# In-projection of a hybrid DeltaNet / neighbourhood-attention layer: values stored four tiles at a time, window copies, a norm's bank, query squares and a triangle mask moved

## The chip, the cores and the metric

The kernel runs on one core of one Trainium2 chip. The metric is the time of one execution in microseconds (us), measured on the device. Times without the profiler are the median of three runs. One more execution was recorded by the hardware profiler, and every view quoted here comes from it.

The core has a matrix engine (TensorE, in the profile PE, its weight loads PEld), a vector engine (DVE), a scalar engine (ACT), a general engine (POOL), and SP, which here only issues DMA transfers. Each engine runs its own list of instructions in order. They wait for each other through semaphores. PE writes its results into banks of an accumulator memory, and the other engines have to copy them out (evacuate them) before a bank is used again.

## The reference

One layer over 1024 latent tokens and 256 context tokens of width 1024. The part that matters here is the input projection, whose columns feed two groups:

```python
px = modulate(rms_norm(x, norm1_w[i]), sh1, sc1) @ w_in[i]
pc = modulate(rms_norm(ctx, norm1_w[i]), csh1, csc1) @ w_in[i]
...
# group A, gated DeltaNet: q, k, v through a short convolution and SiLU
q = l2_normalize(q) * DN_HEAD_DIM ** -0.5
k = l2_normalize(k)
...
m = jnp.where(strict, jnp.einsum("bhncd,bhnmd->bhncm", kb, k) * decay, 0.0)
a_mat = jnp.eye(CHUNK, dtype=f32) + m
u = lax.linalg.triangular_solve(a_mat, v * beta[..., None], left_side=True, lower=True, unit_diagonal=True)
...
# group B, neighbourhood attention
q = rms_norm(q, q_norm_w) * NA_HEAD_DIM ** -0.5
k = rms_norm(k, k_norm_w)
```

Then follow the scans over chunks (group A), the attention over windows of 8 rows (group B), the output projection and a SwiGLU feed-forward network.

## The kernel before

The projection is a list of jobs, worked off in the loop near the end of the printed code. A Block job computes 128 columns of w_in for all tokens; its matmuls are those of L390. The operands are split in two parts each (hh and hl for the tokens, whi and wlo for the weights), and three products are added, so a Block has for each of eight k-steps three products in three pieces of 256, 512 and 512 columns, 72 matmuls (48 in q and nq, which have two pieces). The kinds are k, q, v of group A and nk, nq of group B. A Wide job computes 264 or 256 columns with the tokens as the other operand, ten tiles of 128 tokens each, 24 matmuls L581 per tile: the values of group B (nv, in two halves) and the gate z. The order of jobs is k0 to k3, the values' half 1, nk0 to nk2, the values' half 0, nk3, nq0 to nq2, q0 to q3, then z and v blocks and nq3.

While a job's matmuls run, pieces of other work are put between them, one per step, as Python generators: the convolution's taps of the job before (`taps`, DVE), the finishing of a job (`finish`, transposes and products of keys, L520 and L542), and two backgrounds. `bg2` holds `modulation`, which multiplies the later modulation weights (tile wad, loaded by L213, added up on DVE by L234, summed by PE at L219). `bg` holds `block_inverses` and then `preps`. `block_inverses` builds decay tables (rc on POOL L796, PE L809), transposes them (L828, evacuated by ACT L830), inverts all 32 x 32 diagonal blocks in 30 pairs of steps on DVE (L838, L840), transposes back (PE L850) and stores x_d (L860, L863). `preps` prepares the scan's chunks: it loads e, kk and xc (L890 to L892), masks e to a triangle on POOL (L902), takes its exponential on ACT (L911), and multiplies on PE into bank pr (L920 and L929; L922 evacuates L920's result). A `yield` ends a piece.

What comes out is the order of the instructions on each engine. Banks: blk has four, m and pr two each. The norm of a nk block (L485) squares, sums with a constant matrix and takes logarithm and exponential on ACT; its three pieces all use m.

Small tiles share buffers by tag. Tag kx has three buffers of 640 KB each, for vt, kk, kd (of a k block's finish), kTh, the norm's hl16, and z4. The tag zt has two buffers of one tile of values (128 x 264): ACT copies a tile into it (L592) and SP stores it to nv_d (L595). After the values' half 0, sixteen copies from nv_d to vw_d (L1037) arrange the windows for the attention. All of SP's transfers are issued in one order.

## Time and profile before

| | |
|---|---|
| median of 3 runs | 1564.35 us (1562.84 to 1565.23) |
| profiled execution | 1570.02 us |
| its span (first to last instruction) | 1568.2 us |
| mean granted clock of PE | 0.979 |
| PE busy in the span | 1473.0 us (94%) |
| in-projection | about 37 to 560 us of the span |

The profile lists engines' busy time, their waits (who ended the idle time before an instruction), and the granted clock of PE, in shares of full speed. A timeline row gives the start, the time that a run of like instructions takes, the engine, line, operation, output and input, and in brackets the idle time before it and what ended it. "SPq" rows are transfers issued by SP. L followed by a number is the line of the kernel before; the changed kernel's lines are given where they are used.

### The profile page before, as it was taken

How to read it: one execution, taken by the hardware profiler on the slowest of the kernel's cores; microseconds unless marked ns; L12 is line 12 of the kernel's file. 1: busy time of each engine (PE TensorE's matmuls, PEld its weight loads, DVE VectorE, ACT ScalarE, POOL GpSimd, SP SyncE). 2: the span in 40 equal slices, each digit the busy share in tenths (PEclk: the TensorE clock that was granted, in tenths of full speed). 3: DMA queues.
4: the chain of work that ended last, by engine and by line, in shares of the span. 5: the costliest groups of instructions: out<-in, count | busy, mean ns of one | idle time of the engine just before them, and what ended most of it. 6: DMA issues, size and time to landing. Idle time of an engine off the chain costs nothing.

```text
span 1568.2 us, 23886 instructions
## 1 busy us (share of the span) xinstructions
PE 1473.0 (94%) x8535; PEld 1228.2 (78%) x8535; DVE 1000.3 (64%) x1877; ACT 721.1 (46%) x1406; POOL 185.6 (12%) x253
## 2 busy tenths in 40 slices
PE   3999998999999989899979989999999999999999
PEld 1789777777988868787867878888888888888887
DVE  4866479345264665678986469855555556689642
ACT  5443262684356345566753265333333334445441
POOL 1043710342043300000000000000000000000000
PEclk9999899999999999999998999999999999999999
DMA  9457133654468489899639402533323224698742
GB/s 368 132 191 229 46 85 114 218 166 144 155 217 248 154 226 307 262 287 280 199 97 303 177 29 78 194 108 116 101 101 101 101 101 146 222 369 308 236 153 82
DMA packets 214503, 280.50 MB, mean 179 GB/s; under 512 B 16288, under 2 KB 120304, under 8 KB 213360
## 3 DMA queue, kind: packets, MB, share of 16 engines
q1 hardware_dynamic: 213520, 278.34, 54.4%
q8 instruction: 67, 1.10, 0.3%
q10 hardware_dynamic: 864, 0.63, 0.1%
q14 instruction: 52, 0.43, 0.1%
HBM read 212.02 MB, written 71.08 MB: 181 GB/s over the span
## 4 chain that ended last, share of the span: by engine, by line
PE 67%; ACT 4%; DMA 4%; DVE 3%; issue 2%; POOL 1%; SPq 1%; DVEq 0%; POOLq 0%; ACTq 0%
PE ps L1232 27%; PE ps L1579 13%; PE blk L390 6%; PE ps L1363 4%; PE blk L581 3%; PE sc L318 2%; PE sc L308 2%; PE sc L296 2%; PE pr L929 2%; PE ps L1125 1%; PE ps L1385 1%; PE pr L920 1%; PE ps L1137 1%; PE ps L1142 1%; PE ps L1106 1%
## 5 line engine op out<-in xcount | busy, mean ns | idle before, releaser
L390 PE MATMUL blk<-hh,whi 128*128 128x512 f32 (+1 forms) x416 | 125.5, 396 | 9.9 <-ACT zt L592 5.7
L1293 ACT CAST uhi<-ws 128x512 fp32r<-128x512 f32 x91 | 54.8, 624 | 150.0 <-PE ps L1232 71.3
L1293 ACT CAST uhi<-wq 128x512 fp32r<-128x512 f32 x101 | 60.7, 622 | 135.6 <-issue 61.3
L390 PE MATMUL blk<-hh,wlo 128*128 128x512 f32 (+1 forms) x416 | 117.7, 379 | 2.3 <-POOL wlo L200 2.3
L390 PE MATMUL blk<-hl,whi 128*128 128x512 f32 (+1 forms) x416 | 116.4, 378 | 0.0
L1294 DVE TENSOR_TENSOR ulo<-wq,uhi 128x512 fp32r<-128x512 f32 x101 | 67.4, 688 | 66.1 <-ACT uhi L1293 36.0
L1232 PE MATMUL ps<-hT,uhi 128*128 128x512 f32 x336 | 104.6, 392 | 3.2 <-ACT hT L1411 3.1
L1232 PE MATMUL ps<-lT,uhi 128*128 128x512 f32 x336 | 103.8, 390 | 0.0
L1232 PE MATMUL ps<-hT,ulo 128*128 128x512 f32 x336 | 103.4, 389 | 0.0
L390 PEld LDWEIGHTS blk<-hh,whi 128*128 128x128 f32 x416 | 70.4, 195 | 25.6 <-ACT zt L592 6.0
L1232 PE MATMUL ps<-hB,uhi 128*128 128x512 f32 x288 | 89.7, 392 | 0.0
L390 PEld LDWEIGHTS blk<-hh,wlo 128*128 128x128 f32 x416 | 74.4, 195 | 19.3 <-POOL wlo L200 2.8
L1232 PE MATMUL ps<-lB,uhi 128*128 128x512 f32 x288 | 89.3, 391 | 0.0
L1232 PE MATMUL ps<-hB,ulo 128*128 128x512 f32 x288 | 88.8, 389 | 0.0
L581 PE MATMUL blk<-zhi,hh 128*128 128x264 f32 (+1 forms) x288 | 85.3, 296 | 0.0
L390 PEld LDWEIGHTS blk<-hl,whi 128*128 128x128 f32 x416 | 74.2, 194 | 14.1
L1294 DVE TENSOR_TENSOR ulo<-ws,uhi 128x512 fp32r<-128x512 f32 x91 | 60.8, 687 | 36.1 <-ACT uhi L1293 27.8
L581 PE MATMUL blk<-zhi,hl 128*128 128x264 f32 (+1 forms) x288 | 82.8, 287 | 0.0
L581 PE MATMUL blk<-zlo,hh 128*128 128x264 f32 (+1 forms) x288 | 82.4, 286 | 0.0
L1232 PEld LDWEIGHTS ps<-hT,uhi 128*128 128x128 f32 x336 | 63.1, 189 | 16.9 <-ACT hT L1411 3.5
L1232 PEld LDWEIGHTS ps<-lT,uhi 128*128 128x128 f32 x336 | 63.4, 189 | 13.3
L1232 PEld LDWEIGHTS ps<-hT,ulo 128*128 128x128 f32 x336 | 63.2, 188 | 13.2
(331 smaller groups left out, 3555.0 us busy)
## 6 DMA issues: line engine op xcount, KB each, us to landing
wq<-w_fo SPq DMA_DIRECT2D x99, 256.0 KB
wq<-w_gu SPq DMA_DIRECT2D x88, 256.0 KB
wad<-wa SPq DMA_DIRECT2D x64, 256.0 KB
bt<-rpb SPq DMA_DIRECT2D x64, 192.0 KB
t_d<-g SPq DMA_DIRECT2D x22, 512.0 KB
fr<-t_d SPq DMA_DIRECT2D x44, 256.0 KB
f_d<-g SPq DMA_DIRECT2D x33, 256.0 KB
fr<-f_d SPq DMA_DIRECT2D x33, 256.0 KB
```

Of the source, the lines that this page charges most:

```text
L296: pe.matmul(sc[:, u * 640 + n0:u * 640 + n1], q, ks[i], start=i == 0, stop=i == 1)
L308: pe.transpose(sc[:, u * 640 + j * 128:u * 640 + (j + 1) * 128], bt[:, j * 128:(j + 1) * 128], ident)
L318: pe.matmul(sc[u * ND:u * ND + ND, 1280:1408], vv, pt[:, j * 128:(j + 1) * 128], start=j == 0, stop=j == 4)
L390: pe.matmul(o, ww[:, k], xx[k][:, s], start=k == 0 and j == 0, stop=k == KT - 1 and j == end)
L581: pe.matmul(p[:, :c1 - c0], x[k][:, s], ww[:, k, c0:c1], start=k == 0 and j == 0, stop=k == KT - 1 and j == 2)
L920: pe.matmul(p[:, h * 128:h * 128 + 96], kk[:, h], fx[:, h, s], start=True, stop=True)
L929: pe.matmul(p[q, h * 128:h * 128 + 32 * r], f[:, h, q], y[:, h, s], start=True, stop=True)
L1232: pe.matmul(o, w[wi][:, k], x[xi][:, k], start=first and k == 0 and j == 0, stop=k == n - 1 and j == 2, skip_group_check=True)
L1293: act.copy(hi, self.raw[key])
L1294: dve.tensor_tensor(lo, self.raw[key], hi.bitcast(F32), OP.subtract)
L1363: pe.matmul(o, w[wi][:, k], parts[xi][k][:, s], start=k == 0 and j == 0, stop=k == KT - 1 and j == 2)
L1579: pe.matmul(o[b], w[wi][:, b], F[xn, p][xi], start=n in (0, 1, 5) and p == 0 and j == 0, stop=p == NFB // 2 - 1 and j == 2, skip_group_che ...
```

## The change

1. The values' tiles go into one tile nv4 of four tiles (128 x 4 x 264) of tag kx, stored when four are full (and after the last two): three stores per half instead of ten. The tag zt is gone.
2. The sixteen copies of vw_d become a generator `windows`, stepped twice per k-step in the blocks after the values' half 0.
3. The third piece of a nk norm takes its bank from pr instead of m.
4. The query squares' sum (eight matmuls and a copy, L479 and L481) moves from `norm` to `finish`, behind the load of kTh, with a yield of its own.
5. The triangle mask (L902) moves out of `prep` and is issued one item ahead.
6. Two more yields stand ahead of the loop over `cuts` in `block_inverses`.
7. In the loop of a Wide job `bg2` makes three steps instead of two.

```diff
@@ -474,14 +474,9 @@
                 r = self.r
                 if kind == "q":
                     sp.dma_start(qT_d[:, i], acc[:, t0:])
-                    p = bank()
-                    for c in range(8):
-                        pe.matmul(p[:, c:c + 1], r[:, t0 + c * 128:t0 + (c + 1) * 128], M[C_ONE][:, 0:1],
-                                  start=True, stop=True)
-                    dve.tensor_copy(SQ[:, :, i], p[:, 0:8])
                     return
                 for s0, n in self.segs:
-                    p = bank()
+                    p = bank("pr" if kind == "nk" and s0 >= 768 else "m")
                     pe.matmul(p[:, :n], M[C_BD2], r[:, s0:s0 + n], start=True, stop=True)
                     act.activation(r[:, s0:s0 + n], p[:, :n], AF.Ln, bias=b_eps, scale=1.0 / ND)
                 if kind == "nq":
@@ -529,6 +524,12 @@
                 if kind == "q":
                     kT = cp.tile([128, T], F32, name="kTh", tag="kx", bufs=3)
                     sp.dma_start(kT, kT_d[:, i])
+                    p, r, t0 = bank(), self.r, self.t0
+                    for c in range(8):
+                        pe.matmul(p[:, c:c + 1], r[:, t0 + c * 128:t0 + (c + 1) * 128], M[C_ONE][:, 0:1],
+                                  start=True, stop=True)
+                    dve.tensor_copy(SQ[:, :, i], p[:, 0:8])
+                    yield
                 else:
                     kT = acc
                 if kind in "kq":
@@ -588,11 +589,15 @@
                     nv = 248 if half else 264
                     for t in range(NCH):
                         p = self.wide(t, 0, 264)
-                        vt = cp.tile([128, 264], F32, name="zt", tag="zt", bufs=2)
-                        act.copy(vt[:, :nv], p[:, :nv])
+                        if t % 4 == 0:
+                            vt = cp.tile([128, 4, 264], F32, name="nv4", tag="kx", bufs=3)
+                        act.copy(vt[:, t % 4, :nv], p[:, :nv])
                         if half:
                             act.copy(ab[:, t], p[:, 248:264])
-                        sp.dma_start(nv_d[t * 128:(t + 1) * 128, half * 264:half * 264 + nv], vt[:, :nv])
+                        if t % 4 == 3 or t == NCH - 1:
+                            t0 = t // 4 * 4
+                            sp.dma_start(nv_d[t0 * 128:(t + 1) * 128, half * 264:half * 264 + nv]
+                                         .rearrange("(c p) d -> p c d", p=128), vt[:, :t + 1 - t0, :nv])
                         yield
                     return
                 for t in range(2, NCH):
@@ -801,6 +806,8 @@
                         return out
 
                     nxt = rhs(*cuts[0])
+                    yield
+                    yield
                     yield
                     for i, (d, u0, n) in enumerate(cuts):
                         rcs, nxt = nxt, rhs(*cuts[i + 1]) if i + 1 < len(cuts) else None
@@ -898,9 +905,6 @@
 
                 def prep(n, d, c, kk, xc, e, at):
                     lat = c >= 2
-
-                    pool.affine_select(e, e, pattern=[[0, 4], [1 - 2 * d, 128]], compare_op=OP.is_ge, fill=-1.0e30,
-                                       base=0, channel_multiplier=2 * d - 1)
                     y, fx = ys[n % 4], fxs[n % 2]
                     for b in range(4):
                         q = slice(b * 32, b * 32 + 32)
@@ -931,6 +935,14 @@
                         yield 1
                     stores.append((y_d[d, c], y, tick[0] + 2))
 
+                def triangle(item):
+
+                    (d, _, _, _, e, _), made = item
+                    if not made:
+                        pool.affine_select(e, e, pattern=[[0, 4], [1 - 2 * d, 128]], compare_op=OP.is_ge, fill=-1.0e30,
+                                           base=0, channel_multiplier=2 * d - 1)
+                        item[1] = True
+
                 stores, tick = [], [0]
 
                 def flush(n):
@@ -942,10 +954,13 @@
                 n = 0
                 while live or todo or landing:
                     while len(landing) < 2 and todo and (todo[0][1] < 2 or all(x in done for x in queries)):
-                        landing.append(fetch(*todo.pop(0)))
+                        landing.append([fetch(*todo.pop(0)), False])
                     if landing and len(live) < 3:
-                        live.append(prep(n, *landing.pop(0)))
+                        triangle(landing[0])
+                        live.append(prep(n, *landing.pop(0)[0]))
                         n += 1
+                        if landing:
+                            triangle(landing[0])
                     if not live:
                         yield
                     nxt = []
@@ -968,6 +983,15 @@
         values = inv + 3
         queries = range(turn - 1, later)
         jobs += [Wide("z", 0, zp), Block("v", 0), Wide("z", 1, zp), Block("v", 1), Block("v", 2), Block("v", 3), Block("nq", 3)]
+
+        def windows():
+            vlat = nv_d[CT:].rearrange("(r c) d -> r c d", c=64)
+            for cb in range(4):
+                for ch in range(4):
+                    sp.dma_start(vw_d[:, cb, ch], vlat[4 * ch:4 * ch + 4, BLKS[cb]:BLKS[cb] + 32])
+                    yield
+
+        copies = Background()
 
         def blk(n):
             return jobs[n] if 0 <= n < len(jobs) and isinstance(jobs[n], Block) else None
@@ -1012,7 +1036,7 @@
                         fin = nrm.finish()
                         done.add(n - 1)
                         nrm = None
-                    bg2.step(2)
+                    bg2.step(3)
                     if n < turn:
                         bg.step(2)
                     if n >= turn:
@@ -1026,15 +1050,13 @@
                         next(fin, 0)
                     bg.step(1 if n < turn else 3)
                     bg2.step(1)
+                    copies.step(2)
                 j.evac()
             for _ in fin:
                 pass
             done.add(n - 2)
             if isinstance(j, Wide) and n == values:
-                vlat = nv_d[CT:].rearrange("(r c) d -> r c d", c=64)
-                for cb in range(4):
-                    for ch in range(4):
-                        sp.dma_start(vw_d[:, cb, ch], vlat[4 * ch:4 * ch + 4, BLKS[cb]:BLKS[cb] + 32])
+                copies.add(windows())
             if nrm:
                 nrm.norm()
             if isinstance(j, Block) and j.later is None:
```

Since the order on each engine is a result of all of this, these rows show what stands in it now, at three places. In the rows, a name with a number is one tile of that name, and x4 means four times in a row.

First, SP's list in the values' half 1 (before; wad are the modulation's weights, nv_d the values, kk_d and k_d the keys' products and transposes):

```order
L213 DMA wad<-wa 128x512 x2
L595 DMA nv_d<-zt 128x248
L472 DMA kT_d<-cacc 128x1280
L213 DMA wad<-wa 128x512 x2
L555 DMA kk_d<-kk 1280x1x128
L595 DMA nv_d<-zt 128x248
L213 DMA wad<-wa 128x512 x2
L595 DMA nv_d<-zt 128x248
L213 DMA wad<-wa 128x512 x2
L595 DMA nv_d<-zt 128x248
L528 DMA k_d<-vt 128x10x128
```

and SP's list there in the changed kernel:

```order
L599 DMA nv_d<-nv_957 128x4x248
L213 DMA wad<-wa 128x512 x3
L523 DMA k_d<-vt 128x10x128
L213 DMA wad<-wa 128x512 x3
L472 DMA kT_d<-cacc 128x1280
L556 DMA kk_d<-kk 1280x1x128
L213 DMA wad<-wa 128x512 x2
L599 DMA nv_d<-nv_1142 128x4x248
L523 DMA k_d<-vt 128x10x128
L599 DMA nv_d<-nv_1313 128x2x248
```

The last loads of wad now stand directly behind the store of kk_d, and they are the last two, where four were behind it before; the stores of values are fewer. PE's list at the end of that job, before (L219 sums a modulation product, L542 multiplies keys, L390 begins nk0):

```order
L581 MATMUL blk<-zlo,hh_418 128x264
L542 MATMUL m<-cacc 128x128 x6
L219 MATMUL m<-ones,acc_1165 128x1 x4
L390 MATMUL blk<-hh_134,whi 128x256
L390 MATMUL blk<-hh_134,whi 128x512 x2
```

and the same sum, the last of the modulation, in the changed kernel (L515 is L520 of before):

```order
L582 MATMUL blk<-zlo,hh_418 128x264
L515 MATMUL m<-cst,cacc 128x128 x2
L219 MATMUL m<-ones,acc_1071 128x1 x4
L582 MATMUL blk<-zhi,hh_134 128x264
L582 MATMUL blk<-zhi,hl_135 128x264
```

It moved from the job's end to the end of its eighth tile, ahead of two more tiles.

Second, PE's list in the last k-steps of block nk2, before (L828 is the last of four groups of transposes that feed the block inverses):

```order
L390 MATMUL blk<-hl_415,whi 128x256
L390 MATMUL blk<-hl_415,whi 128x512 x2
L390 MATMUL blk<-hh_414,wlo 128x256
L390 MATMUL blk<-hh_414,wlo 128x512 x2
L828 MATMUL m<-cst,WK 80x128 x8
L390 MATMUL blk<-hh_416,whi 128x256
L390 MATMUL blk<-hh_416,whi 128x512 x2
```

and in the changed kernel, where L835 is L828 of before and L480 is L485:

```order
L390 MATMUL blk<-hh_418,wlo 128x256
L390 MATMUL blk<-hh_418,wlo 128x512 x2
L835 MATMUL m<-cst,WK 80x128 x8
L480 MATMUL pr<-cr,cst 128x512
L480 MATMUL m<-cr,cst 128x256
L480 MATMUL m<-cr,cst 128x512
L582 MATMUL blk<-zhi,hh_134 128x264
```

The feeding transposes moved back by two k-steps (18 matmuls L390), the last of them to the block's end; the norm's one piece has a bank pr.

Third, PE's list in block q2, before (the query squares of q0):

```order
L390 MATMUL blk<-hh_418,wlo 128x512 x2
L390 MATMUL blk<-hh_134,whi 128x512 x2
L390 MATMUL blk<-hl_135,whi 128x512
L479 MATMUL m<-ones,cr 128x1 x8
L390 MATMUL blk<-hl_135,whi 128x512
L390 MATMUL blk<-hh_134,wlo 128x512 x2
```

and in the changed kernel (L529 is L479 of before, L543 is L542):

```order
L390 MATMUL blk<-hl_141,whi 128x512 x2
L390 MATMUL blk<-hh_140,wlo 128x512 x2
L529 MATMUL m<-ones,cr 128x1 x8
L390 MATMUL blk<-hh_412,whi 128x512 x2
L390 MATMUL blk<-hl_413,whi 128x512 x2
L390 MATMUL blk<-hh_412,wlo 128x512 x2
L543 MATMUL m<-cacc,kTh 128x128 x4
```

They moved from the third matmul of the block to behind its fourth k-step.

## The prediction

> **What bounds the kernel now.** I read the engines' totals first, then what TensorE (PE) waited for in the in-projection, then the clock by stretches of 40 us there.
>
> ```profile
> PE 1473.0 (94%) x8535; PEld 1228.2 (78%) x8535; DVE 1000.3 (64%) x1877; ACT 721.1 (46%) x1406; POOL 185.6 (12%) x253
> ```
>
> PE is busy for 94% of the span, so only its own idle time and a lowered clock can be won without removing matmuls, and the change removes none. Everything it moves runs between 113 and 560 us. PE's waits from 37 to 560 us (released by; total, times, longest):
>
> ```profile
> PE blk L390 <- ACT zt L592: 5.7, 1, 5.7
> PE m L485 <- ACT cr L486: 5.2, 4, 1.5
> PE pr L929 <- ACT kk L922: 3.5, 2, 3.0
> PE m L479 <- ACT cr L464: 3.4, 1, 3.4
> PE m L219 <- DVE modp L221: 2.1, 1, 2.1
> PE m L809 <- POOL rc L796: 2.0, 1, 2.0
> ```
>
> These six make 21.9 us, and each belongs to one edit. A wait also costs what comes after it. Two groups of the same one-column matmuls in PE's timeline, sixteen records each (start, busy, what, idle before), and two rows of the block matmuls:
>
> ```profile
> 360.66 3.57 PE L479 MATMUL m<-ones,cr 128*128 128x1 f32 x16 [3.36 <-ACT cr L464]
> ...
> 376.38 0.62 PE L390 MATMUL blk<-hh,whi 128*128 128x512 f32 x2
> 376.83 0.62 PE L390 MATMUL blk<-hl,whi 128*128 128x512 f32 x2
> ...
> 377.74 1.84 PE L479 MATMUL m<-ones,cr 128*128 128x1 f32 x16
> ```
>
> After a gap of 3.36 us they took 3.57 us, without a gap 1.84: half speed. The stretches of 40 us show how much (the number behind the engines is the granted clock, PEclk):
>
> ```profile
> 120.00:160.00 40.00, 36.79 (x291) 36.06 (x290) 26.79 (x39) 12.20 (x37) 15.79 (x20) 0.95 0.67 207
> 160.00:200.00 40.00, 36.65 (x172) 29.42 (x172) 20.20 (x44) 14.15 (x26) 24.44 (x23) 0.93 0.18 59
> 240.00:280.00 40.00, 34.35 (x203) 30.45 (x203) 33.76 (x38) 9.09 (x13) 2.41 (x1) 0.91 0.33 117
> 360.00:400.00 40.00, 39.34 (x223) 35.11 (x224) 20.27 (x18) 14.03 (x20) 9.53 (x4) 0.91 0.45 151
> 440.00:480.00 40.00, 36.97 (x313) 34.00 (x313) 24.20 (x35) 25.53 (x60) 19.65 (x31) 0.91 0.70 220
> ```
>
> 40 us times the missing clock is 2.0, 2.8, 3.6, 3.6 and 3.6 us, and each of these stretches holds one of the long waits. So a long wait costs itself and 2 to 3.6 us of half speed.
>
> **The change part by part**, in the times of the profiled execution (1570.02 us; span 1568.2), which is 5.67 us above the unprofiled median of 1564.35.
>
> *First values block (half 1, 113 to 157 us).* The new tiles nv4 take buffers of tag kx, which has three, shared with vt, kk and kd. SP, ACT, POOL, DVE and PE rows of before:
>
> ```profile
> 126.33 0.57 SPq L555 DMA_DIRECT2D kk_d<-kk  x1
> 132.59 0.43 SPq L528 DMA_DIRECT2D k_d<-vt  x1
> 142.68 0.56 SPq L555 DMA_DIRECT2D kk_d<-kk  x1
> 144.15 1.87 SPq L213 DMA_DIRECT2D wad<-wa  x2
> 137.64 0.59 ACT L522 COPY vt<-m 128x512 f32<-128x512 f32 x1 [0.50 <-DMA k_d<-vt]
> 135.62 2.93 POOL L547 TENSOR_TENSOR kd<-kk,cst 128x1280 f32<-128x1280 f32 x1 [9.32 <-ACT kk L543]
> 151.36 3.11 DVE L234 SCALAR_TENSOR_TENSOR acc<-wad,sc,acc 128x512 f32<-128x512 f32 x4 [7.62 <-DMA wad<-wa]
> 127.48 1.05 PE L542 MATMUL m<-cacc 128*128 128x128 f32 x8
> ...
> 143.17 0.38 PE L520 MATMUL m<-cst,cacc 128*128 128x128 f32 x2
> 154.62 1.02 PE L219 MATMUL m<-ones,acc 128*128 128x1 f32 x8 [2.12 <-DVE modp L221]
> 156.73 1.44 PE L390 MATMUL blk<-hh,whi 128*128 128x256 f32 x3 [1.09 <-ACT kk L543]
> ```
>
> A 640 KB store freed its buffer 137.64 − 132.59 = 5.0 us after its issue. Now job k2's vt lies where k1's kk was, so its copies wait for the store issued at 126.33: about 131, and PE's L542 of 127.48 comes about 3.4 us later. k2's kd then waits for k2's k_d store (from the same 5.0 us, an estimate: until 141.5), and takes 2.9 us; the zeroing behind it ends near 146, and the kk_d store is issued then instead of at 142.68. The last two wad loads stand behind it on SP. Before, such loads were used 151.36 − 144.15 = 7.2 us after issue; now that is about 153 to 154. bg2.step(3) moves the last L219 on PE from the block's end to the place of the L520 that ran at 143.17, so PE arrives there near 146 and waits until about 154. Behind L219 are still 48 matmuls L581 and the transposes, 7.4 us. Job nk0 starts near 161.5 instead of 156.73: **+4.8**, with half speed behind the wait as before. Ends: −4.1 if the buffers come free in time (2.1 and the 2.0 of clock), +9.8 if the loads also wait out one more store (5.0).
>
> *Two more yields, first consequence.* POOL's pieces for L809 were late because of a cast of the values weights:
>
> ```profile
> 185.44 3.69 POOL L574 TENSOR_TENSOR zlo<-wraw,zhi 128x1056 fp32r<-128x1056 f32 x1
> ```
>
> The last L809 now stands 18 L390 later on PE (about 4 us, as two L390 start every 0.45 us), which covers the 2.0. With the 2.8 of clock that is up to −4.8; some of the lost clock may stem from nk0's start: **−3.0** (−4.8 to 0).
>
> *Norm piece in bank pr.* The first three blocks' third piece no longer waits for a bank m: −1.4 for the first; the next two are in the following sum.
>
> *Values four at a time, and the block inverses.* ACT's wait for nv_d stores and with it PE's 5.7 goes. But the inverse's chain on DVE is next (30 pairs, then the row where PE picks up its result):
>
> ```profile
> L838 DVE TENSOR_TENSOR tt<-N 80x120 f32<-80x120 f32 (+14 forms) x30 | 27.5, 915 | 7.1 <-ACT N L830 6.1
> L840 DVE TENSOR_TENSOR N<-N,tt 80x120 f32<-80x120 f32 (+14 forms) x30 | 25.4, 847 | 0.9
> 213.50 1.07 ACT L830 COPY N<-m 80x512 f32<-80x512 f32 x2 [1.56 <-PE m L828]
> 274.99 0.28 DVE L840 TENSOR_TENSOR N<-N,tt 80x120 f32<-80x120 f32 x1
> 281.84 0.34 PE L850 MATMUL m<-cst,N 80*128 80x80 f32 x2
> ```
>
> From the last L830 (214.57) to the chain's end (275.27) it is 60.7 us, and PE came 6.6 us after that. Now the feeding matmuls L828 stand 18 L390 later (4.2 us): end 279.5. PE reaches L850, itself moved 16 L390 (3.6 us) back, at 281.84 + 3.6 − 5.7 − 3.6 (clock) − 1.5 − 1.0 (the two norms) = 273.6, so it **waits about 6 us for DVE**, and restarts at half speed (2.5). Against 285.4 before: 279.8 + 2.5, **−3.1**. Ends: −11.8 without the new wait, 0 if ACT brings the result later still.
>
> The sixteen copies to vw_d aren't spread by SP's order: four, three and nine stand behind the three stores. They waited before too, beside PE's work, and their cover is the whole stretch to the next weights:
>
> ```profile
> 264.48 13.23 SPq L1037 DMA_DIRECT2D vw_d<-nv_d  x6
> ```
>
> *nk3's third piece.* The fourth wait (1.3) goes, but with the scan's products taking pr first, the piece is 86 L390 later on PE. ACT's and DVE's steps on it release the buffer cacc, and nq1's evacuation L423 needs that buffer and must be done before q0's first L390:
>
> ```profile
> 294.56 1.12 PE L485 MATMUL m<-cr,cst 128*128 128x512 f32 x2 [1.27 <-ACT cr L486]
> ...
> 300.82 1.26 ACT L498 CAST hl<-cacc 128x1280 f16<-128x1280 f32 x1 [1.62 <-DVE cacc L493]
> ...
> 316.25 1.09 ACT L423 ACTIVATE cacc<-blk 128x512 f32<-128x512 f32 x2
> ...
> 332.48 1.03 PE L390 MATMUL blk<-hh,whi 128*128 128x512 f32 x2
> ```
>
> Before, the evacuation was done 332.48 − 317.3 = 15.1 us ahead. Now the piece stands only 6 L390 and some small products (estimate 3.6 us) ahead of q0. From the piece to the cast's end took 302.1 − 294.6 = 7.5 us, and DVE's subtraction and half the evacuation add some 1.9: 9.4 us. So PE **waits about 5.8 us** there, and a little at a lower clock: 6.5 (0 to 10), **+5.2** net (−1.3 to +8.7).
>
> *Query squares.* Eight matmuls and one DVE copy go from norm to finish, behind the kTh load; no DMA moves with them. In PE's row they now come 21 L390 later (4.8 us), longer than the wait of 3.36: 3.4 and 3.6 of clock go, and I keep 1 for the first: **−6.0** (−7.0 to −3.4).
>
> The Trainium skill ("TensorE: Matmul & The Clock Gate", section "HAM oscillation — how this bites in real kernels") says that PE must have no idle gap over about 3.4 us. By it only the 5.7 us wait would lower the clock, and the 3.6 would not be there to win; this trace disagrees, with half speed right behind 3.36 us and a clock of 0.93 around a wait of 2.0. The sum goes by the rows.
>
> *Triangle.* The mask L902 stood behind a weight cast on POOL, the exponential behind the mask on ACT, and the copy that PE waited for behind that:
>
> ```profile
> 448.13 3.33 POOL L200 TENSOR_TENSOR wlo<-wraw,whi 128x1024 fp32r<-128x1024 f32 x1 [2.03 <-ACT whi L199]
> 452.26 0.40 ACT L911 ACTIVATE e<-e,GN 128x128 f32<-128x128 f32 x1 [3.40 <-POOL e L902]
> ```
>
> Now the mask is ahead of that cast and L922 no longer behind a waiting L911: 3.0 and 3.6 of clock, **−6.6** (to 0 if POOL's copies ahead of it wait for a store).
>
> Sum: 4.8 − 3.0 − 1.4 − 3.1 + 5.2 − 6.0 − 6.6 = −10.1. Profiled 1559.9, unprofiled **1554.2 us**, 0.6% less.
>
> **Rivals.**
> - *The kx buffers come free in time and nq1's evacuation isn't late.* First block −4.1, L809 −4.8, nk3 −1.3, squares −7.0, the rest as above: −28.3, 1536.0 us. For it: the DMA engines were only 0.67 busy there (the figure behind PEclk), so stores might land sooner. Against: the 5.0 us row. Without DVE's bound too it would be 1527.
> - *New waits for old, nothing won.* The mask still waits (0 instead of −6.6) and the squares' clock isn't regained (−3.4 instead of −6.0): −0.9, 1563.5 us. For it: vw_d is still bunched, and DVE's chain shows how near the next wait lies.
> - *Slower: stores in the first values block.* If in the three-buffer ring vt, nv4 and kd each wait out a store one after another, at 5.0 us each with PE idle, four of them make 20 us. The gain without that block is 14.9; above a loss of 18.0 there the change is over 0.2% slower, and with 20 it is at 1569.5. Against it: ten tiles give PE 30 us of work beside them.
> - *The clock drops only past 3.4 us:* L809, squares and triangle then give their waits alone, −1.2, −2.4 and −3.0 instead of −3.0, −6.0 and −6.6, in sum −1.1: 1563.3 us. The half speed of L479 behind 3.36 us speaks against it. It is the Trainium skill's rule named above.
>
> **How the numbers follow.** Forecast 0.58 (its own range 1547 to 1561), first rival 0.16, no gain 0.13, slower 0.11, clock 0.02. Faster by over 0.2% (3.1 us, about what a measurement of this kernel can tell from no change) 0.74, within 0.15, slower 0.11. The range 1537 to 1565 takes in the forecast, the cases without gain and the nearer part of the first rival; it leaves out the slower one and half the first.
>
> **What would show it.** Right: PE's list has no zt, no L485 and no 3.4 us row for the squares; it has a wait of 4 to 8 us on DVE at the moved L219 and one of 3 to 6 us at L850's new line, one of 4 to 8 us in front of q0, and clocks near 1.00 around 360 and 450 us. Wrong: L219 without a wait (first rival), a wait over 10 us at the first block (slower), or nq1's evacuation done before PE reaches q0.

## The result, and the profile after

The changed kernel takes 1569.78 us (median of 15 runs, 1564.43 to 1575.60) against 1565.23 (1558.24 to 1568.27) for the kernel before: ratio 1.0037, 95% interval 1.0026 to 1.0048. It is slower by 0.37%, about 5.8 us by the ratio (the two medians differ by 4.6). The prediction said 0.6% faster and is wrong in sign, and the median lies above its range.

The waits that the change aimed at are gone. PE's waits of the changed kernel from 37 to 560 us (waiting, released by; total, times, longest):

```profile
PE m L219 <- DVE acc L234: 7.4, 1, 7.4
PE m L857 <- DVE N L851: 5.7, 1, 5.7
PE m L857 <- ACT WK L859: 3.5, 1, 3.5
PE pr L933 <- DVE y L934: 2.8, 4, 1.2
...
PE pr L924 <- DVE y L934: 2.2, 1, 2.2
PE pr L924 <- DVE kk L916: 2.0, 1, 2.0
...
PE m L543 <- ACT vt L517: 1.6, 1, 1.6
PE m L816 <- POOL rc L801: 1.0, 1, 1.0
...
PE blk L390 <- ACT cacc L423: 0.8, 1, 0.8
```

No row is left for the values' copies, the key norms or the query squares, and the longest wait for the copy kk of L926 (L922 before) is 1.0 us instead of 3.0. But L219 waits 7.4 us where it waited 2.1, and the pickup of the inverse (L857, formerly L850) waits 5.7 and 3.5 us where it waited not at all. The same stretches of 40 us as in the prediction, and the one between 280 and 320 us (PEclk is the third figure from the end):

```profile
120.00:160.00 40.00, 31.07 (x241) 30.65 (x241) 22.60 (x33) 9.69 (x28) 12.96 (x19) 0.91 0.67 208
160.00:200.00 40.00, 38.33 (x214) 32.82 (x212) 20.13 (x47) 10.75 (x25) 22.52 (x21) 0.96 0.16 51
...
280.00:320.00 40.00, 29.01 (x128) 22.63 (x129) 14.38 (x20) 17.34 (x34) 11.55 (x18) 0.87 0.54 181
320.00:360.00 40.00, 37.46 (x208) 27.10 (x207) 17.39 (x27) 35.72 (x74) 19.07 (x33) 0.87 0.62 177
360.00:400.00 40.00, 40.00 (x212) 34.26 (x211) 22.86 (x20) 20.91 (x28) 8.98 (x5) 1.00 0.49 157
...
440.00:480.00 40.00, 36.78 (x338) 32.70 (x338) 25.08 (x39) 25.46 (x56) 20.79 (x32) 1.00 0.75 243
```

The clock that was low around 260, 360 and 450 us is now low in two stretches from 280 to 360 us: 40 us times 0.13, twice, is 10.4 us, where the kernel before had lost nothing. In steps of 10 us this is not one long stretch but three places:

```profile
280.00:290.00 10.00, 4.56 (x24) 3.91 (x24) 5.83 (x13) 1.63 (x4) 0.00 (x0) 0.66 0.39 141
290.00:300.00 10.00, 6.49 (x28) 4.72 (x27) 2.74 (x2) 5.83 (x11) 2.39 (x1) 0.83 0.18 57
...
320.00:330.00 10.00, 10.00 (x71) 7.65 (x70) 3.44 (x7) 8.02 (x26) 5.36 (x13) 0.83 0.57 177
330.00:340.00 10.00, 8.60 (x73) 5.79 (x70) 4.31 (x8) 8.79 (x13) 4.40 (x6) 1.00 0.68 211
340.00:350.00 10.00, 8.86 (x27) 6.11 (x28) 4.41 (x6) 9.32 (x16) 5.32 (x10) 0.66 0.78 205
```

The first (5.1 us lost) is at the two waits of the pickup, the second (1.7) behind the wait of 2.0 us for the copy L916, the third (3.4) behind several short waits in front of q0.

The two profiled executions have the same span, 1568.2 us, although the medians differ: that of before took longer (1570.02 us) than any of its 15 unprofiled executions. So I compare stretches between marks that both have. From the first wide matmul of the values' half 1 to the attention's first wait (573.29 before, 579.55 after, less the starts at 113.77 and 115.50) it is 459.5 us before and 464.1 us after: 4.5 us more, which is close to the medians' 4.6. The views of this stretch, before and after (PE's busy time is the figure behind the length):

```profile
113.77:573.29 459.52, 433.97 (x2857) 371.05 (x2856) 256.36 (x356) 223.25 (x434) 139.64 (x170) 0.97 0.53 167
```

```profile
115.50:579.55 464.05, 431.84 (x2856) 369.39 (x2855) 258.88 (x356) 222.82 (x434) 139.39 (x170) 0.97 0.54 165
```

PE is idle for 25.6 us before and 32.2 us after, at the same mean clock. So the change has moved the low clock and not reduced it, and has added waiting. By parts, from PE's timeline:

| stretch on PE | before | after | difference | predicted |
|---|---|---|---|---|
| values' half 1, nk0 to nk2 (to the start of half 0) | 104.4 | 108.9 | +4.5 | +0.4 |
| half 0, nk3, nq0 (to the norm behind nq0) | 72.8 | 71.9 | −0.8 | −3.1 |
| nq1, nq2, q0 (to the norm behind q0) | 52.9 | 61.2 | +8.3 | +5.2 |
| q1 and half of q2, with the first squares | 26.6 | 19.8 | −6.9 | −6.0 |
| from there to the attention | 202.8 | 202.2 | −0.6 | −6.6 |

The norm behind nq0 stands five L390 later in the changed kernel, for which 1.2 us are taken off its start (297.46). The differences make 4.5 us, the predicted ones −10.1. The first row is uncertain by some 4 us: r8, one of the runs r1 to r16 of the next section, has the instructions of the kernel before up to there and took 99.9 us, while r3, r7 and r13, with those of the changed kernel, took 108.7 to 110.5.

### The profile page after: what moved, and what is told of

Its sections match the earlier page's. It is cut to its first block, busy times and chain, and to the rows that moved or that the text cites. A ratio compares the mean times of both kernels' runs of the same rounds, so it can differ in the third digit from the quotient of the medians.

```text
span 1568.2 us, 23877 instructions
## 1 busy us (share of the span) xinstructions
PE 1466.6 (94%) x8535; PEld 1224.7 (78%) x8535; DVE 1002.6 (64%) x1877; ACT 720.4 (46%) x1406; POOL 184.7 (12%) x253
## 4 chain that ended last, share of the span: by engine, by line
PE 69%; DMA 12%; DVE 7%; ACT 5%; issue 2%; POOL 2%; SPq 2%; ACTq 0%; DVEq 0%; POOLq 0%
PE ps L1254 26%; PE ps L1601 13%; PE blk L390 8%; PE ps L1385 3%; PE blk L582 2%; PE sc L318 2%; DMA wad<-wa 2%; PE sc L308 2%; PE sc L296 2%; DMA wraw<-w_conv 1%; PE pr L933 1%; PE ps L1147 1%; PE ps L1407 1%; DMA fraw<-w_conv 1%; PE pr L924 1%
## 5 line engine op out<-in xcount | busy, mean ns | idle before, releaser
L390 PE MATMUL blk<-hh,whi 128*128 128x512 f32 (+1 forms) x416 | 124.5, 395 | 4.3 <-ACT whi L199 1.6
L390 PE MATMUL blk<-hh,wlo 128*128 128x512 f32 (+1 forms) x416 | 119.2, 381 | 2.3 <-POOL wlo L200 2.3
L390 PE MATMUL blk<-hl,whi 128*128 128x512 f32 (+1 forms) x416 | 116.4, 376 | 0.0
L390 PEld LDWEIGHTS blk<-hh,wlo 128*128 128x128 f32 x416 | 74.5, 195 | 19.1 <-POOL wlo L200 2.9
L390 PEld LDWEIGHTS blk<-hh,whi 128*128 128x128 f32 x416 | 70.8, 195 | 20.2 <-issue 2.6
L390 PEld LDWEIGHTS blk<-hl,whi 128*128 128x128 f32 x416 | 73.4, 191 | 14.2 <-issue 0.5
```

The lines of the kernel that those rows point to most:

```text
L390: pe.matmul(o, ww[:, k], xx[k][:, s], start=k == 0 and j == 0, stop=k == KT - 1 and j == end)
```

## The experiments

Times are medians beside runs of the kernel before on the same chip; "nk0 starts" is counted from the first wide matmul (43.0 us before and 40.3 in r8, whose instructions are the same up to there; 53.1 us after, and 52.9 to 54.3 in r3, r7 and r13).

**What costs the first values block?** Two runs take one part back each. The first:

```diff
+                        if half:
+                            vt = cp.tile([128, 264], F32, name="zt", tag="zt", bufs=2)
...
+                            sp.dma_start(nv_d[t * 128:(t + 1) * 128, 264:264 + nv], vt[:, :nv])
```

> The changed kernel, but the values' half 1 goes back to its own two single tiles (tag zt, ten stores); half 0 keeps nv4 on kx. Theory (the kx ring costs the first values block): job k2's vt copies no longer wait for a store, the kk_d store of k2 is issued 4 to 5 us sooner, PE's wait at the last L219 falls from 7.4 us to under 4, and nk0 starts 5 to 9 us sooner than in the changed kernel (168): stage end 4 to 8 us sooner, time 1562 to 1566. Rival (the third step of bg2 puts L219 too early, whatever the ring does): L219 still waits 5 us or more, and nk0 starts less than 3 us sooner.

Measured (run r1): 1565.57 us, ratio 1.0014 (1.0003 to 1.0024). PE's wait at L219 is longer than before the edit:

```profile
PE m L219 <- DVE acc L234: 7.9, 1, 7.9
```

and nk0 starts at 50.9, only 2.2 us sooner: the rival. The buffers of kx are not what makes L219 wait. They do cost something near 131 us: PE's wait of 1.6 us at L543 in the changed kernel, for copies to vt that wait 7.8 us for the store of kk_d, is not in this run. The second run:

```diff
-                    bg2.step(3)
+                    bg2.step(2)
```

> The changed kernel with two steps of the modulation per tile instead of three; the ring stays. Theory of the ring: the loads of wad are still late behind kk_d, so nk0 starts less than 3 us sooner. Rival (the early L219): L219 stands at the block's end again, its wait falls under 3 us and nk0 starts 5 us or more sooner.

Measured (run r2): 1561.83 us, ratio 0.9987 (0.9974 to 1.0000): half a per cent less than the changed kernel. nk0 starts at 46.8, 6.2 us sooner, and L219 no longer waits for its data. The same edit alone, on the kernel before:

```diff
-                    bg2.step(2)
+                    bg2.step(3)
```

> The kernel before with only the third step of the modulation per tile. Theory (the third step puts the last L219 ahead of its loads, whatever the buffers do): a wait of 5 to 8 us at L219, nk0 starts 4 to 9 us later than before the change, time 1566 to 1571 against 1563.5. Rival (the loads are only late through the kx ring): the wait at L219 stays under 3 us and the time within 2 us of the kernel before.

Measured (run r12): 1571.46 us against 1562.86, ratio 1.0049 (1.0035 to 1.0062), nk0 starts at 50.9. Its waits, and the rows of SP and DVE at that place:

```profile
PE m L219 <- DVE acc L234: 7.3, 1, 7.3
```

```profile
145.05 0.56 SPq L555 DMA_DIRECT2D kk_d<-kk  x1
145.71 1.89 SPq L213 DMA_DIRECT2D wad<-wa  x2
```

```profile
151.00 1.54 DVE L234 SCALAR_TENSOR_TENSOR acc<-wad,sc,acc 128x512 f32<-128x512 f32 x2 [4.35 <-DMA wad<-wa]
```

No buffer is shared here, and the loads of wad still stand behind kk_d's store, are used 5.3 us after their issue, and PE waits 7.3 us: the third step alone brings that wait. The data of L219 comes no later for it: L219 began 40.9 us after the first wide matmul in the kernel before (154.62 less 113.77), 39.9 in the changed kernel and 39.1 here. It now stands ahead of two tiles, which wait with it.

**nk3's third norm piece.**

```diff
-                    p = bank("pr" if kind == "nk" and s0 >= 768 else "m")
+                    p = bank("pr" if kind == "nk" and i < 3 and s0 >= 768 else "m")
```

> The changed kernel, but nk3's third norm piece (and only that one) takes its bank from m again. Theory (the piece, late behind the scan's products in pr, delays nq1's evacuation and so q0): the piece is early again on PE, the stretch from the end of nq0 to the first norm behind q0, 8.3 us longer than before the change in the profiles, is within 3 us of before, a wait of about 1.3 us at L480 returns, time 1562 to 1567. Rival (the scan's chain itself is late because x_d is late): the stretch stays 5 us or more longer.

Measured (run r3): 1565.58 us, ratio 1.0013 (0.9997 to 1.0028), 0.24% less than the changed kernel. The stretch from nq0's norm to that behind q0 is 55.7 us (296.17 to 351.89); between the same two rows the changed kernel takes 60.1 (297.46 to 357.54). That is 4.4 us less; with the 1.2 us of the table it is still some 4 us longer than before the change, instead of 8, between what theory and rival had said. No wait of 1.3 us came back. PE's rows of the changed kernel in front of q0:

```profile
331.02 1.02 PE L480 MATMUL pr<-cr,cst 128*128 128x512 f32 x2
...
338.24 0.41 PE L933 MATMUL pr<-y,kk 128*32 128x32 f32 x8 [0.66 <-ACT kk L926]
339.12 0.61 PE L933 MATMUL pr<-y,kk 128*32 128x64 f32 x8 [0.47 <-DVE y L934]
340.34 1.25 PE L933 MATMUL pr<-y,kk 128*32 128x96 f32 x8 [0.61 <-DVE y L934]
342.40 0.79 PE L390 MATMUL blk<-hh,whi 128*128 128x512 f32 x1 [0.81 <-ACT cacc L423]
```

None of these four waits is in r3, and its clock is 1.00 from 330 to 350 us. So the piece's place costs about 4 us, in short waits and in the half speed behind them. The wait of 2.0 us for L916 stays (2.8 us here), and so does the low clock at the pickup (0.79 from 280 to 320 us).

**The inverse's chain.** First one yield instead of three:

```diff
                     nxt = rhs(*cuts[0])
                     yield
-                    yield
-                    yield
```

> The changed kernel with one yield ahead of the loop over cuts, as before the change. Theory (the two yields start the inverse's chain on DVE two k-steps later and make PE wait 5.7 us for it): that wait falls to 0.5 to 3 us and the 3.5 us wait for ACT behind it shrinks too; the wait for rc on POOL returns with about 2 us; time 1564 to 1569. Rival (the chain's length of 60 us decides, whatever its start): the two waits together stay above 7 us.

Measured (run r4): 1573.74 us, ratio 1.0073 (1.0052 to 1.0094). The wait for DVE's chain hardly changed, although the chain starts 18 L390 sooner:

```profile
PE m L855 <- DVE N L849: 5.4, 1, 5.4
```

PE's pickup moved forward by sixteen L390 as well. The wait for rc is 2.0 us again, and the kernel is slower, so the two yields were worth having. The theory of the late start fell.

**Three parts back at once, then a later pickup.** Half 1 in single tiles, nk3's piece in m, and two steps, all three edits as above:

> The changed kernel with three parts undone at once: values' half 1 in its own single tiles, nk3's third norm piece in m, two modulation steps per tile. If the three costs seen one by one (3.6, 3.6 and 7.4 us against the changed kernel) lie at different places and add up, the time is 1553 to 1557 against 1563.5 for the kernel before; if they overlap (the wait at one place covers the other), it is near the best single one, 1560 to 1563.

Measured (run r5): 1558.98 us against 1563.76, ratio 0.9959 (0.9945 to 0.9974). That is 0.78% less than the changed kernel, while the three singly make 0.97%, and it lies between the two ranges expected. With these intervals it is open whether the costs overlap. Then four more yields at the end of the chain:

```diff
                 dve.memset(flat[:P, :, 0:1024:33], 1.0)
-                yield
+                for _ in range(5):
+                    yield
```

> The run before (three parts undone), and in addition four more yields between the end of the inverse's chain on DVE and the transposes on PE that pick up its result. Theory (PE comes to the pickup 5.7 us before DVE's chain is done, because it no longer stalls for the values): the wait of 5.7 us falls under 1, and the half speed behind it goes; 5 to 9 us less in the profile up to the end of nq0, of which the scan's preparation, now later, may give some back. Rival (PE only waits later for x_d and the scan's first products): less than 2 us won by the start of z0.

Measured (run r6): 1561.52 us (1554.82 to 1570.49), ratio 0.9979 (0.9961 to 0.9997), not to be told from the run before. The wait is 5.7 us again, because the transposes stand at the same place in PE's list as without the yields: the number of yields did not move them. With 22 of them they did move:

```diff
-                for _ in range(5):
+                for _ in range(22):
```

> The run with three parts undone, and 22 yields at the end of the inverse's chain instead of one: on PE the first transposes that pick the result up now stand 19 L390 later (about 4.3 us) and the four groups are a k-step apart (four yields had left PE's order as it was). Theory (the place of the pickup in PE's order costs 5.7 and 1.9 us of waiting and the half speed behind it): the wait falls to 1 to 2 us, the clock between 240 and 320 us is 0.95 or more, and the time is 4 to 9 us less than that run (1559.0 against 1563.8 for the kernel before): 1550 to 1555. Rival (x_d is now later still, so the scan's first products wait for it): won by the end of nq0, lost again by the start of z0, time 1557 to 1561.

Measured (run r9): 1559.45 us, ratio 0.9989 (0.9975 to 1.0003), 0.30% more than with one yield. Nothing was won, but not by the rival's way: the wait at the pickup is gone, and one of 14.1 us stands before it. PE, ACT and SP rows of this run:

```profile
286.88 2.07 PE L480 MATMUL m<-cr,cst 128*128 128x512 f32 x2 [14.10 <-ACT cr L481]
```

```profile
283.01 1.04 ACT L199 CAST whi<-wraw 128x1024 fp32r<-128x1024 f32 x1 [20.51 <-DMA wraw<-w_nqk]
```

```profile
249.83 20.77 SPq L997 DMA_DIRECT2D vw_d<-nv_d  x9
270.69 2.37 SPq L198 DMA_DIRECT2D wraw<-w_nqk  x1
```

Nine copies to vw_d stand on SP in a row and take 20.8 us to issue. The load of the next weights stands behind them, ACT's cast waits for it, and all of ACT's work behind the cast waits too. The changed kernel has the same rows:

```profile
260.73 20.85 SPq L991 DMA_DIRECT2D vw_d<-nv_d  x9
281.68 2.37 SPq L198 DMA_DIRECT2D wraw<-w_nqk  x1
```

```profile
294.09 1.04 ACT L199 CAST whi<-wraw 128x1024 fp32r<-128x1024 f32 x1 [4.02 <-DMA wraw<-w_nqk]
295.04 0.74 ACT L859 COPY WK<-m 128x320 f32<-128x320 f32 x2
```

The evacuation L859 on which PE's second wait at the pickup (3.5 us) hangs follows that cast on ACT. In the kernel before, the same cast waited for PE and not for the load:

```profile
290.69 1.05 ACT L199 CAST whi<-wraw 128x1024 fp32r<-128x1024 f32 x1 [3.10 <-PE blk L390]
```

The 3.5 us are those of one execution; in r1, r2, r3 and r7, with the copies and the pickup in the same place, this second wait is 1.7 to 2.0 us.

**The same question with a smaller set** (the kernel before with the squares, the norm piece of nk0 to nk2, and half 0 alone four at a time), with one and with 23 yields:

> The kernel before with the query squares moved, the third norm piece of nk0 to nk2 in pr, and only the values' half 0 stored four tiles at a time; one yield, two modulation steps, the mask as before. Theory (ACT's wait for the stores covered the inverse's chain): the wait of 5.2 to 5.7 us for the values' copies goes and one of 5 to 6 us for DVE's chain stands at the pickup, so that up to the end of nq0 it isn't more than 3 us shorter than with the squares alone (1559.6). Rival (my prediction's: PE's pickup waits only because the two yields made the chain late): the wait at the pickup is under 2.5 us, 1551 to 1555.

Measured (run r10): 1552.50 us against 1562.86, ratio 0.9935 (0.9920 to 0.9950). One wait has taken the other's place, with one yield ahead of the cuts and two steps of the modulation:

```profile
PE m L860 <- DVE N L854: 5.4, 1, 5.4
```

It is faster than I had expected of it, 0.36% less than the squares alone. The profiles don't place this gain: the stage takes 447.8 us here and 445.5 in r8, whose profiled execution (1556.86 us) lies 2.8 us under its median.

> The run before with 23 yields at the end of the inverse's chain: the pickup stands 29 L390 later on PE (about 6.5 us), in groups apart. Theory: no wait over 1 us at the pickup, clock near 1.00 between 240 and 320 us, 4 to 8 us less than the run before, 1549 to 1554. Rival (later x_d): no gain over the run before.

Measured (run r11): 1562.21 us, ratio 0.9995 (0.9980 to 1.0009): the gain is lost to a wait of 13.8 us for L481, as in the run with 22 yields.

**The copies on another queue.** To take the copies out of SP's list without removing them:

```diff
-                    sp.dma_start(vw_d[:, cb, ch], vlat[4 * ch:4 * ch + 4, BLKS[cb]:BLKS[cb] + 32])
+                    pool.dma_start(vw_d[:, cb, ch], vlat[4 * ch:4 * ch + 4, BLKS[cb]:BLKS[cb] + 32])
```

In the changed kernel:

> The changed kernel with the sixteen copies to vw_d issued from POOL's queue instead of SP's. Theory (nine copies in a row hold SP for 20.8 us, so the next weights w_nqk are loaded late, ACT's cast L199 waits for them with the inverse's evacuations L859 behind it, and PE waits 3.5 us): the weight load on SP is issued before 275, that wait falls under 1.5 us, 2 to 5 us less in the stage. Rival (ACT's evacuations are slow by themselves): the wait stays above 2.5 us. If POOL is held by the copies, PE waits for its L200 instead.

Measured (run r13): 1563.18 us against 1565.53, ratio 0.9987 (0.9972 to 1.0001), half a per cent less than the changed kernel. POOL and SP rows:

```profile
256.56 5.38 POOL L991 DMA_DIRECT2D vw_d<-nv_d  x8 [14.46 <-DMA nv_d<-nv]
...
266.01 0.68 POOL L991 DMA_DIRECT2D vw_d<-nv_d  x1 [0.21 <-issue]
```

```profile
272.09 0.60 SPq L198 DMA_DIRECT2D wraw<-w_nqk  x1
```

The copies are issued by 266.7 instead of 281.6, the weights' load at 272.1 instead of 281.7, and no row of PE waiting for L859 is left. The wait for DVE's chain is still 5.7 us. The gain of 0.50% is more than the wait that went; what else it comes from is open. The control:

> The best run so far (squares, norm piece, half 0 four at a time; 1552.5 against 1562.9 for the kernel before) with the copies on POOL's queue. Its PE didn't wait for ACT at the pickup, so the theory gives no more than 2 us; a rival that the copies' traffic itself disturbs gives no change either.

Measured (run r14): 1553.12 us, ratio 0.9937 (0.9916 to 0.9957): no change, as PE hadn't waited for ACT there. Now the later pickup with the copies out of the way, on the larger and the smaller set:

> The run with the pickup 19 L390 later, in which PE stood 14.1 us for nk2's norm because ACT's cast waited 20.5 us for the weights behind the copies, now with the copies on POOL's queue. Theory: the 14.1 us wait falls under 2 us and the pickup's wait stays under 2 us: the stage is 8 to 14 us shorter than in that run, 1548 to 1554. Rival (DVE's chain holds PE there in any case): a wait of 5 us or more stays between 270 and 300 us.

Measured (run r15): 1549.63 us against 1565.53, ratio 0.9901 (0.9879 to 0.9923). PE's longest waits of this run:

```profile
PE pr L939 <- ACT kk L932: 3.8, 2, 3.4
PE blk L390 <- POOL wlo L200: 2.3, 2, 1.5
PE m L219 <- DVE modp L221: 2.1, 1, 2.1
PE pr L930 <- DVE kk L922: 2.1, 1, 2.1
```

> The same on the smaller set (squares, norm piece, half 0, pickup 29 L390 later): its 13.8 us wait falls under 2 us, no wait over 1 us at the pickup, 1544 to 1552 against 1562.9 for the kernel before. Rival: a wait of 5 us or more stays, or the scan's first products take back what was won: 1553 or more.

Measured (run r16): 1549.88 us, ratio 0.9905 (0.9883 to 0.9926), with full clock where the changed kernel lost 10.4 us:

```profile
240.00:280.00 40.00, 39.20 (x226) 33.79 (x224) 36.77 (x39) 10.92 (x17) 13.49 (x15) 1.00 0.53 155
280.00:320.00 40.00, 36.17 (x187) 28.01 (x188) 14.74 (x15) 28.27 (x55) 12.38 (x27) 1.00 0.60 197
320.00:360.00 40.00, 38.45 (x222) 29.08 (x221) 28.39 (x31) 31.91 (x62) 25.74 (x25) 1.00 0.62 192
```

No wait for the chain over 0.3 us is left in either, and the 14 us are gone. On the smaller set all four cases were run: either edit alone gains nothing over one without them (0.9995 and 0.9937 against 0.9935), both together 0.30%. So the place of the pickup in PE's list was the cause of the first wait, and the copies on SP that of the second. Both of these beat both kernels. The Trainium skill ("DMA: Bandwidth & Descriptors", section "Issuing engines are not separate DMA queues") says that another issuing engine saves only the sequencer's time to issue, which it calls usually small relative to the transfer. Here it was not small: in the changed kernel it brought the weights' load 9.6 us forward (281.7 to 272.1), and with the later pickup it took away PE's wait of 14 us. Nor was it all: the load was used 12.3 us after its issue behind the copies on SP (270.69 to 283.01 in the run with 22 yields), and at most 7.2 us after it with the copies on POOL (263.16 to 270.36 in the same kernel), where the cast waited for PE. Whether the other queue did this or the longer time since the last copy, no run separates.

**The mask and the squares.** The mask back in prep, in the changed kernel:

```diff
                 def prep(n, d, c, kk, xc, e, at):
                     lat = c >= 2
+                    pool.affine_select(e, e, pattern=[[0, 4], [1 - 2 * d, 128]], compare_op=OP.is_ge, fill=-1.0e30,
+                                       base=0, channel_multiplier=2 * d - 1)
```

> The changed kernel with the triangle mask back inside prep, issued when its item starts. My prediction's step (the early mask takes away 3.0 us of waiting and 3.6 of clock): the stretch from the squares of q0 to the attention's first wait becomes 5 us or more longer than in the changed kernel (204 us there), a wait of 2 to 4 us of L933 for the copy kk returns. Rival (the scan's products wait for DVE's copies in any case, and the mask only chose where): the stretch changes by less than 2.5 us.

Measured (run r7): 1569.10 us against 1563.76, ratio 1.0033 (1.0018 to 1.0047), like the changed kernel. The stretch is 201.4 us (374.83 to 576.19), 2.5 shorter, and the only wait for the copy kk in it is 0.4 us. The mask's move gains nothing that these runs can tell. Then the squares alone, in the kernel before:

> The kernel before with only the query squares moved to finish. Prediction's step: the wait of 3.4 us at the squares and the half speed behind it go: 1556 to 1560 against 1563.5. Rival (what it gains there another wait takes later in the block of z or v): within 2 us of the kernel before.

Measured (run r8): 1559.64 us, ratio 0.9971 (0.9955 to 0.9987). The wait of 3.4 us is gone, and so is the one of 3.0 us near 450 us, with the mask where it was; the clock is 1.00 there and from 360 to 400 us:

```profile
440.00:480.00 40.00, 39.48 (x381) 36.48 (x380) 25.79 (x42) 30.32 (x73) 17.98 (x24) 1.00 0.83 256
```

## Why the prediction was wrong

Between the −10.1 us forecast and the +4.5 measured in the stage lie 14.6: 6.0 of them are in the last row of the table (the triangle), 4.1 in the first, 3.1 in the third and 2.3 in the second; the squares gained 0.9 more than forecast.

- **First values block (predicted +4.8, measured +10.1).** The place and length of the wait were right (L219, about 8 us predicted, 7.4 measured), its cause wrong. I put the late loads down to the shared buffers; r12 has the wait without them, and r1 keeps it when half 1 has its own. The failed step is the term's mechanism: bg2.step(3) calls L219 some 7 us before its data, which comes when it came before, buffers or not. The size was also off. From L219's start to nk0's I took 7.4 us at full speed; it took 13.2, above all because L219, the next 24 matmuls and the products behind them ran at half speed (155.35 to 163.57: 24 matmuls in 5.4 us, the last 24 in 3.0). That cost some 3.5 us ahead of nk0, and PE's wait of 1.6 us at L543 was not in the sum.
- **L809 and the first norms (−3.0, −1.4).** The waits went: 2.0 to 1.0 us, and L485's to none. With the block above, the stretch to the values' half 0 is 4.5 us longer where 0.4 was predicted, so these two and the restart of nk0 gave back 5.6 us where 4.4 were predicted. r4 supports the yields' part: without them the wait of 2.0 us returns and the kernel is 0.36% slower.
- **Values and inverse (−3.1, measured −0.8).** The wait for DVE's chain was right to 0.3 us (about 6, measured 5.7). What I missed is the second wait, 3.5 us. The failed step is "The sixteen copies to vw_d ... their cover is the whole stretch to the next weights". The cover was PE's own stall: before, the cast of these weights waited for PE; now the cast waits for the load behind the copies (294.09, where it stood at 290.69).
- **nk3's third piece (+5.2; r3 gives 4.4 in its stretch, 0.24% in the median).** The size was near, by luck: the path was right, two of its lengths were not. nq1's evacuation does come late behind the piece, and q0 can begin only 11.4 us after it (331.02 to 342.40; 9.4 predicted). But PE waits only 0.8 us for it, not 5.8, because PE needs 10.6 us from the piece to q0 where I estimated 3.6: eight groups of the scan's products stand between them, three of which wait 0.5 to 0.7 us for copies. The half speed behind these waits (0.66 from 340 to 350 us) is the larger part. The rest of the +8.3 is what the prediction did not have: the scan's first products wait 2.0 us for the copy L916, with half speed behind it.
- **Query squares (−6.0, measured −6.9).** The wait and the half speed behind it went as forecast. But r8, the squares alone, gains 0.29%, 4.5 us (2.0 to 7.0), although it also loses the wait of 3.0 us and the low clock near 450 us, which the forecast priced at 6.6 more. So the two terms, 12.6 us together, were worth 4.5 in the median. I had read their prices in the one profiled execution, 1570.02 us where the median is 1565.23; where the rest goes is open (one new wait in r8 is 1.8 us for kTh).
- **Triangle (−6.6, measured −0.6).** The failed step is that the early mask removes the wait. The 3.0 us and the low clock went, but r8 loses them without the mask's move, by the squares' move alone; r7 has no such wait with the mask back; and r12, with neither edit, keeps it (3.0 us). The waits of the scan's products for DVE (2.2, and 2.8 in four) stand in their place in the changed kernel. What moved these was not tried by itself.
- **The rivals.** The one that named the sign, stores in the first values block, had the wrong mechanism (the buffers); its place was right. The second, new waits for old, is the nearest to what happened, though it had the mask still waiting and no loss. The one by which the clock drops only past 3.4 us is refuted further: the clock is 0.83 from 320 to 330 us behind a wait of 2.0 us, and 0.66 from 340 to 350 us behind waits of under 1 us.

The runs do not split the 0.37% into parts that add up: r2 and r13 each take off 0.50%, r1 and r3 some 0.24% each. r10 is faster than r5 by 0.24%, with the chain's wait in both. r5 has three more parts of the change (copies spread by `windows`, mask, two yields), and in its profile two waits that r10 lacks, 1.9 us for ACT at the pickup and 3.3 us of the scan's products for DVE. No run takes these parts one by one.

## What to carry to other kernels

When a stall is removed, ask which waits ended inside it: here a chain on DVE, a weight load behind bunched copies and their cast had all been hidden by PE's stall of 5.7 us, and the first of them came back with nearly the same length (5.4 to 5.7 us). Where a planner makes the order, a piece that has been moved by yields is moved only if the rows of the engine's list say so: four yields changed nothing, and copies that the code spreads stood in a row of nine. Work that is drawn forward (the third modulation step) can reach PE before its loads do. And a price read in one execution is that execution's price: check it against the median of a run that makes that edit alone.

## What the runs showed of the hardware that I had not expected

Nine copies of 256 KB each (DRAM to DRAM) in a row held SP's queue for 20.8 us, 2.3 us each, while the first four of them took 2.8 us together (from 240.63). The load behind the nine took about 12 us from its issue (281.68) to the cast that waited for it (294.09). From POOL's queue the last twelve copies were issued in 10.1 us (256.56 to 266.69), where SP took 23.6 (257.96 to 281.58). The 2.0 us wait for rc was followed by half speed in the profile of before (the next L390 in groups of three took 1.27 us instead of 0.74), but not in r8, where a wait of 1.99 us left a clock of 1.00: a gap of about 2 us lowers the clock in some executions and not in others. And three gaps of 0.5 to 0.7 us within 2.8 us (337.58 to 340.34) and a fourth of 0.8 us behind them went with a clock of 0.66 from 340 to 350 us of the changed kernel. The Trainium skill ("TensorE: Matmul & The Clock Gate", section "What's actually happening") has PE's recent activity judged in windows of about 3.4 us that run freely, so that where a gap falls in its window would matter. No run here shows those windows.
